# Routed experts in groups of four 32-slot tiles: 26 groups for 28, and a second PSUM bank for combine

## The chip, the cores and the metric

The kernel runs on one core of one Trainium2 chip. The metric is the device time of one execution in microseconds (us). Three runs of the kernel before took 1636.47, 1637.51 and 1638.44 us; the median is 1637.51. A profile was taken of one further execution, and all rows below are from it.

## The reference, cut to what matters

The reference is two transformer blocks on 256 tokens of width 1024, all in float32. The first block ends in a mixture of experts, and only that part is touched here:

```python
scores = sigmoid(xt @ w_router)                      # 256 tokens, 64 experts
choice = scores + router_bias                        # best 4 of 8 groups of experts, then top 8 experts
wts    = scores[eidx] / sum * 2.5                    # 8 weights per token: 2048 assignments
for each expert e, on the rows routed to it:
    ye = (silu(x @ w_gate_e[e]) * (x @ w_up_e[e])) @ w_down_e[e]     # 1024 -> 256 -> 1024
    routed[rows] += ye * w
return routed + swiglu(xt, w_gate_sh, w_up_sh, w_down_sh)            # a shared expert for all tokens
```

Each expert has 1 MB of gate and up weights for the first half of the width, 1 MB for the second, and 1 MB for down: 192 MB for the 64. The counts of tokens per expert are known only when the router has run. The second block has attention over a memory (its values need a projection of 256 by 1024, `mem_v`) and a second mixture of 16 larger experts, whose weights (about 200 MB) are streamed at the end of the kernel.

## The kernel before, in words

**Sorting the experts.** The kernel ranks the 64 experts by their counts on the chip: a position for each, the largest counts first. Four experts (0, 1, 62 and 63, `FIRST`) are put ahead of all others, since their weights are loaded while the router still works. The capacity of a position is fixed when the kernel is built: 64 slots for the first four, 128 for the next four (`N1`), 64 for the next 32 (`N2`), 32 for the remaining 24. If an expert has more tokens than its position has slots, a flag turns on a branch (lines 1137 to 1178) that runs all 64 experts once more on what was left over.

**Groups.** TensorE's 128 columns are 128 slots. A group fills them with one expert of 128 slots, two of 64 or four of 32, placed side by side by `tile_position`. There are 4 groups of one expert, 18 of two and 6 of four, 28 in all. `_group_pairs` puts them into 14 pairs and sets the order: the four pairs that come first have two experts in each of their groups (groups 0 to 7), then pairs of a four with a one and pairs of two twos take turns. The order on TensorE is the order of the code (`manual_schedule`).

**One group** (class `Group`, lines 960 to 1064, called from the loop at 1084) does this on TensorE: `gate_up` (line 1021; 8 steps over the width, each with one matmul for each tile, N = 512, into the single bank u); then the four quarters of `combine` of the group before (lines 1054 and 1055, bank c, which DVE adds into `y1` at line 1064), mixed with the gather of half of the next pair's rows (lines 956 and 957, bank g, copied by ScalarE), the transpose of the activations (`flip`, line 1032), `place` (line 991, which slot each token takes) and `weigh` (line 1003, the routing weight of each slot), these three in bank t; then `down` (line 1045, two halves in the two y banks), whose result ScalarE and DVE split into a high and a low part (lines 214 and 215).

**Spare work.** Work that no group needs at once is a generator, `pieces`, that issues one matmul for each step: the shared expert's gate (16 steps), the memory values `mem_v` (64 steps, line 731), the shared expert's up (16) and down (16). Twenty steps are issued during the routing, five while the first pair is gathered, and the rest by `piece(fills)` at two places in each group's middle; `FILL` says how many at each: none in a group of one expert, 2 in a group of two, 4 in a group of four. Their bank is d, of which there is one; line 735 (ScalarE) or line 749 (DVE) empties it.

**Loads.** SP issues the expert weights in 1 MB transfers (line 929) in the order in which groups need them: the first halves of the group's gate/up weights, the second halves, the down weights. They go to a ring of buffers ("lanes"), ten at first. A load waits until TensorE's last matmul on the buffer's old contents is done. `pieces` hands over more buffers when their contents are no longer needed: two after `mem_v`, two after the shared up, one after the shared down. The loads of group i+1 stand ahead of group i's matmuls in the code. When the last group's loads are issued, five loads of the next block's `w_in2` follow them on the same queue (line 1096). Three transfers of 1 MB for the spare work are issued by ScalarE's queue ("park", line 652).

The eight PSUM banks of this stage are d 1, t 2, g 1, u 1, y 2, c 1.

Of the kernel before, what the change touches and what calls it, by code (L numbers as in the profile page):

```python
# [21 lines left out]
P = 128  # L22
# [6 lines left out]
FILL = {1: 0, 2: 2, 4: 4}  # L29


# [3 lines left out]
NF, N1, N2 = len(FIRST), 4, 32  # L35
CAP1, CAP2, CAP4 = 128, 64, 32


def _group_pairs():
    s = [(NF + i, 1) for i in range(N1)]  # L40
    p = [(2 * i, 2) for i in range(NF // 2)] + [(NF + N1 + 2 * i, 2) for i in range(N2 // 2)]
    q = [(NF + N1 + N2 + 4 * i, 4) for i in range((N_EXP - NF - N1 - N2) // 4)]
    out = []
    while s or p or q:
        g = []
        for lst in (p, p) if len(out) < 4 or not q or (len(out) % 2 and len(p) - 2 >= len(q) - len(s)) else (q, s or p):
            if lst:
                g.append(lst.pop(0))
        if g:
            out.append(g)  # L50
    return out
# [4 lines left out]
def body(tc, I, out):  # L56
# [76 lines left out]
    slotc = lambda n: col("iotac" if n == 1 else f"slot{n}", 1)  # L133
    own = lambda n: col(f"own{n}", 2 * n)
# [561 lines left out]
    open_banks(b2, "b2", d=1, t=2, g=1, u=1, y=2, c=1)  # L696
# [7 lines left out]
    def shared(ps, w, a):  # L704
        w = w.rearrange("p (k n) -> p k n", k=KD)
        for k in range(KD):
            nc.tensor.matmul(ps[:, :T + 1], w[:, k, a * P:(a + 1) * P], hx[:, k], start=(k == 0), stop=(k == KD - 1))
            yield
# [11 lines left out]

    mem_v = None

    def values():
        nonlocal mem_v
        mem_v = big(5, [P, 2, D], F32, "mem_v")
        for c in range(4):
            w = parked.popleft().rearrange("p (k n) -> p k n", k=KD)
            for b in range(2):
                ps = bank("d")
                for k in range(KD):  # L730
                    nc.tensor.matmul(ps[:, :256], hm[:, k, b * P:(b + 1) * P], w[:, k], start=(k == 0),
                                     stop=(k == KD - 1))
                    if k < KD - 1:
                        yield
                nc.scalar.activation(mem_v[:, b, 256 * c:256 * c + 256], ps[:, :256], AF.Copy, scale=rmc[:, b:b + 1])
                if b == 0:
                    yield
            yield park

    def shared_down():  # L740
        w = parked.popleft().rearrange("p (f n) -> p f n", f=2)
        for j in range(4):
            ps = bank("d").rearrange("p (a t) -> p a t", a=2)
            for a in range(2):
                o = (2 * j + a) * P
                for f in range(2):
                    nc.tensor.matmul(ps[:, a], w[:, f, o:o + P], sgl[:, f], start=(f == 0), stop=(f == 1))
                    yield
            nc.vector.tensor_add(y1[:, 2 * j:2 * j + 2], ps, y1[:, 2 * j:2 * j + 2])

    def pieces():
        for a in range(2):
            yield from shared(gate[a], shg, a)
        yield from values()
        add_lanes(2, 10)
        w = parked.popleft()
        for a in range(2):
            ps = bank("d")
            yield from shared(ps, w, a)
            shared_act(1, a, ps)  # L760
        add_lanes(11, 7)
# [16 lines left out]
    for b in range(2):  # L778
        for q in range(2):
            ps = bank("cdug"[2 * b + q])  # L780
# [142 lines left out]
    groups = [(i0, n, pi, g) for pi, gp in enumerate(GROUP_PAIRS) for g, (i0, n) in enumerate(gp)]  # L923
# [8 lines left out]
    def slots(pi):  # L932

        G = pe.tile([P, 2, 2, P], F32R, name="G", tag="G")
        for g, (i0, n) in enumerate(GROUP_PAIRS[pi]):
            cap = P // n
            for b in range(2):
                last = nc.vector.tensor_tensor(
                    G[:, b, g].rearrange("p (e s) -> p e s", e=n),
                    iota[:, None, :cap].to_broadcast([P, n, cap]),  # L940
                    rkS[:, b, i0:i0 + n, None].to_broadcast([P, n, cap]), op=ALU.is_equal)
# [18 lines left out]
    class Group:  # L960


        def __init__(self, i, i0, n, pi, g):
            self.i, self.i0, self.n, self.pi, self.g = i, i0, n, pi, g
            self.cap = P // n

        def tp(self, j):
            return dict(tile_position=(0, self.cap * j)) if self.n > 1 else {}

        def load(self):  # L970
            self.regs, self.gu, self.wd = [], [], []
            if self.i0 < NF:
                es = FIRST[self.i0:self.i0 + self.n]
# [4 lines left out]
            for j in range(self.n):  # L978
                with tc.issue_after(issued[-8]) if len(issued) >= 8 else nullcontext():
                    self.regs.append(nc.sync.value_load(idx[0:1, self.i0 + j:self.i0 + j + 1], min_val=0, max_val=63))  # L980
                first.append(eload(I["w_gu"], self.regs[j], 0))
# [3 lines left out]
        def place(self):  # L985

            i0, n, cap = self.i0, self.n, self.cap
            ps = bank("t")
            for j in range(n):
                c = permb[:, i0 + j:i0 + j + 1]  # L990
                nc.tensor.matmul(ps[cap * j:cap * (j + 1), :T],
                                 bass.AP(tensor=c.tensor, offset=c.offset, ap=[c.ap[0], [0, cap]]), rkTb,
                                 start=True, stop=True, **self.tp(j))
            self.S = pe.tile([P, T], F32R, name="S", tag="S")
            nc.vector.tensor_scalar(self.S, ps[:, :T], slotc(n), 0.0, op0=ALU.is_equal, op1=ALU.add)

        def weigh(self):

            i0, n = self.i0, self.n
            G = Gs[self.pi][:, :, self.g]  # L1000
            ps = bank("t")
            for b in range(2):
                nc.tensor.matmul(ps[:, :2 * n], G[:, b], wS[:, b, i0:i0 + n].rearrange("p e u -> p (e u)"),
                                 start=(b == 0), stop=(b == 1))
            self.wsl = pe.tile([P, 1], F32, name="wsl", tag="wsl")
            if n > 1:
                wm = pe.tile([P, 2 * n], F32, name="wm", tag="wm")
                nc.vector.tensor_mul(wm, ps[:, :2 * n], own(n))
                nc.vector.reduce_sum(self.wsl, wm, axis=AX)
            else:  # L1010
                nc.vector.reduce_sum(self.wsl, ps[:, :2], axis=AX)

        def gate_up(self):
            cap = self.cap
            xg = xg_of[self.pi][:, :, self.g * P:(self.g + 1) * P]
            pg = bank("u")
            for half in range(2):
                ws = [w.rearrange("p (k n) -> p k n", k=4) for w in self.gu[half]]
                for k in range(4):
                    for j in range(self.n):  # L1020
# [15 lines left out]
        def down(self):  # L1036
            cap = self.cap
# [3 lines left out]
            for h in range(2):  # L1041
                py = bank("y")
                for f in range(2):
                    for j in range(self.n):
                        nc.tensor.matmul(py[cap * j:cap * (j + 1)], self.aT[:, f, cap * j:cap * (j + 1)],  # L1045
                                         wd[j][:, f, h * 512:(h + 1) * 512], start=(f == 0), stop=(f == 1),
                                         **self.tp(j))
# [28 lines left out]
    with tc.manual_schedule(engines={mybir.EngineType.PE}):  # L1076
# [5 lines left out]
        piece()  # L1082
        gr[0].weigh()
        for i, u in enumerate(gr):
# [23 lines left out]
            fills = FILL[u.n]  # L1108

# [6 lines left out]
            piece(fills)  # L1116
# [7 lines left out]
            piece(fills)  # L1124
# [611 lines left out]
def layout(inp):  # L1736
# [47 lines left out]
    for n in (2, 4):  # L1784
        cap = P // n
        addv(f"slot{n}", (pidx % cap)[:, None].astype(np.float32))
        addv(f"own{n}", (pidx[:, None] // cap == np.arange(2 * n)[None] // 2).astype(np.float32))
# [49 lines left out]
```

## Time and profile before

| | us |
|---|---|
| median of three runs | 1637.51 |
| profiled execution | 1637.62 |
| its span, first to last instruction | 1635.8 |
| TensorE busy (PE) | 1419.8 |
| VectorE busy (DVE) | 615.4 |
| ScalarE busy (ACT) | 431.8 |
| moved by DMA | 524.76 MB, 321 GB/s over the span |

How to read it: the span leaves out 1.8 us before the first and after the last instruction. PE's busy time counts modelled ends of pipelined matmuls, so how long a step took is read from the start of one instruction to the start of the next. The granted clock is a share of 2.4 GHz; 0.50 is 1.2 GHz. The routed experts take the stretch from 318 us (the first `gate_up`) to 818 us (the end of the last `down`); the first mixture's routing lies just before, the second block after it.

### The profile page before, as it was taken

What the parts mean: (1) busy time and instruction counts of PE and PEld (TensorE: products, weight loads), DVE (VectorE), ACT (ScalarE), POOL (GpSimd) and SP (SyncE); (2) the same over time, 40 slices, a digit from 0 to 9 for tenths busy, and PEclk for the clock granted to TensorE, in tenths of its full rate; (3) what the DMA queues carried; (4) which work ended last, traced back from release to release, by engine and by line L of the source; (5) the groups of instructions that cost most, each with busy time, mean ns of one, the idle gap of its engine ahead of it and who ended that gap; (6) DMA issues with size and microseconds to landing.
All of it is one profiled execution on the core that took longest, in us unless ns stands there. A gap on an engine that the chain in (4) does not pass through costs nothing. (4 is left out here: it accounts for less than half of the span.)

```text
span 1635.8 us, 23949 instructions
## 1 busy us (share of the span) xinstructions
PE 1419.8 (87%) x9780; PEld 903.9 (55%) x9780; DVE 615.4 (38%) x1111; ACT 431.8 (26%) x756; POOL 101.8 (6%) x155
## 2 busy tenths in 40 slices
PE   6999999899999999999878999999796767777664
PEld 5778898554555555444378889999441121121121
DVE  6433654532223233333376566675321111111112
ACT  4453454211111111112165444454210000000001
POOL 1010101200000000000021110011200000000001
PEclk9999999999999999999988999999899777777876
DMA  8885746198999999999944345575399999999995
GB/s 327 340 348 211 297 167 223 68 376 342 383 390 403 416 418 421 415 420 420 420 162 143 115 143 203 196 284 217 140 420 421 421 421 420 421 421 421 421 421 215
DMA packets 74161, 524.76 MB, mean 321 GB/s; under 512 B 8282, under 2 KB 9890, under 8 KB 10562
## 3 DMA queue, kind: packets, MB, share of 16 engines
q1 hardware_dynamic: 72848, 519.35, 79.1%
q10 hardware_dynamic: 1202, 3.87, 0.6%
q8 instruction: 77, 1.26, 0.3%
q14 instruction: 34, 0.28, 0.0%
HBM read 521.01 MB, written 2.17 MB: 320 GB/s over the span
## 5 line engine op out<-in xcount | busy, mean ns | idle before, releaser
L215 DVE TENSOR_TENSOR whl<-w,whl 128x1024 fp32r<-128x1024 f32 x156 | 195.5, 1257 | 143.1 <-ACT whl L214 140.5
L221 PE MATMUL ps_d<-h_hi,whl 128*128 128x256 f32 x1216 | 225.6, 284 | 1.1 <-ACT whl L214 1.1
L214 ACT CAST whl<-w 128x1024 fp32r<-128x1024 f32 x156 | 162.8, 1048 | 167.5 <-PE ps_d L221 141.1
L1021 PE MATMUL ps_u<-w,xg 128*64 128x512 f32 (+2 forms) x1024 | 200.5, 594 | 3.1 <-DMA w<-in_w_gu 3.1
L221 PEld LDWEIGHTS ps_d<-h_hi,whl 128*128 128x128 f32 x1216 | 189.2, 189 | 6.8 <-ACT whl L214 2.8
L221 PE MATMUL ps_d<-h_lo,whl 128*128 128x256 f32 x608 | 171.6, 282 | 0.0
L1586 PE MATMUL ps_u<-w,xgb 128*32 128x512 f32 x512 | 95.7, 822 | 51.1 <-DMA w<-in_w_gu 51.1
L1021 PEld LDWEIGHTS ps_u<-w,xg 128*64 128x64 f32 (+2 forms) x1024 | 64.9, 130 | 134.9 <-issue 127.2
L221 PEld LDWEIGHTS ps_d<-h_lo,whl 128*128 128x128 f32 x608 | 114.2, 188 | 1.5 <-issue 1.3
L1586 PE MATMUL ps_u<-w,xga 128*32 128x512 f32 x512 | 95.7, 708 | 19.1 <-DMA w<-in_w_gu 19.0
L1655 PE MATMUL ps_y<-w,aT 128*32 128x256 f32 x1024 | 84.3, 470 | 28.6 <-DMA w<-in_w_down 24.4
L1045 PE MATMUL ps_y<-w,aT 128*64 128x512 f32 (+2 forms) x512 | 105.0, 605 | 0.0
L1054 PE MATMUL ps_c<-S,yy 128*128 128x256 f32 x224 | 74.0, 352 | 20.9 <-DVE y L1064 13.3
L1064 DVE TENSOR_TENSOR y<-ps_c,y 128x512 f32<-128x512 f32 x100 | 68.6, 686 | 53.2 <-PE ps_c L1055 53.2
L1643 DVE SCALAR_TENSOR_TENSOR act<-ps_u,wsl,sl 128x256 f32<-128x256 f32 x16 | 7.7, 483 | 211.8 <-ACT sl L1633 211.8
L1586 PEld LDWEIGHTS ps_u<-w,xgb 128*32 128x32 f32 x512 | 12.7, 124 | 123.7 <-DMA w<-in_w_gu 118.0
L1027 DVE SCALAR_TENSOR_TENSOR act<-ps_u,wsl,sl 128x256 f32<-128x256 f32 x28 | 13.6, 484 | 176.5 <-ACT sl L1025 176.5
L1633 ACT ACTIVATE sl<-ps_u 128x256 f32<-128x256 f32 x16 | 6.1, 383 | 275.2 <-PE ps_u L1586 275.1
L1655 PEld LDWEIGHTS ps_y<-w,aT 128*32 128x32 f32 x1024 | 33.5, 129 | 74.9 <-DMA w<-in_w_down 44.2
L1054 PEld LDWEIGHTS ps_c<-S,yy 128*128 128x128 f32 x224 | 42.8, 191 | 50.3 <-issue 21.2
L214 ACT CAST yy<-ps_y 128x512 fp32r<-128x512 f32 x56 | 32.8, 585 | 116.0 <-PE ps_y L1045 116.0
L215 DVE TENSOR_TENSOR yy<-ps_y,yy 128x512 fp32r<-128x512 f32 x56 | 38.7, 691 | 57.7 <-ACT yy L214 57.7
(493 smaller groups left out, 2281.7 us busy)
## 6 DMA issues: line engine op xcount, KB each, us to landing
w<-in_w_gu SPq DMA_DIRECT2D x256, 1024.0 KB, 16.3
w<-in_w_down_e SPq DMA_DIRECT2D x64, 1024.0 KB, 11.0
w<-in_w_down SPq DMA_DIRECT2D x64, 1024.0 KB, 19.8
w<-in_w_in SPq DMA_DIRECT2D x42, 1024.0 KB, 6.2
w<-in_w_ada SPq DMA_DIRECT2D x24, 1024.0 KB, 10.0
w<-in_w_mem_kv SPq DMA_DIRECT2D x4, 1024.0 KB, 13.9
w<-in_w_out SPq DMA_DIRECT2D x4, 1024.0 KB, 7.3
w<-in_w_conv_out SPq DMA_DIRECT2D x4, 1024.0 KB, 4.9
```

The lines of the kernel that those rows point to most:

```text
L214: nc.scalar.copy(hi, src)
L215: eng.tensor_sub(lo, src, hi.bitcast(F32))
L221: nc.tensor.matmul(region, l, r, start=(start and u == 0), stop=(stop and u == 2), skip_group_check=True)
L1021: nc.tensor.matmul(pg[cap * j:cap * (j + 1)], xg[:, 4 * half + k, cap * j:cap * (j + 1)], ws[j][:, k], start=(half == 0 and k == 0), stop= ...
L1027: nc.vector.scalar_tensor_tensor(self.act, pg[:, 256:], self.wsl, sl, op0=ALU.mult, op1=ALU.mult)
L1045: nc.tensor.matmul(py[cap * j:cap * (j + 1)], self.aT[:, f, cap * j:cap * (j + 1)], wd[j][:, f, h * 512:(h + 1) * 512], start=(f == 0), st ...
L1054: nc.tensor.matmul(ps[:, a], self.yy[:, 0, k * P:(k + 1) * P], self.S, start=True, stop=False)
L1064: nc.vector.tensor_add(y1[:, 2 * q:2 * q + 2], ps, y1[:, 2 * q:2 * q + 2])
L1586: mm = nc.tensor.matmul(pg[32 * j:32 * j + 32], xg[k][:, 32 * e:32 * e + 32], w[:, 512 * j:512 * j + 512], start=(k == 0), stop=(k == KD - ...
L1633: silu = nc.scalar.activation(sl, pg[:, :256], AF.Silu)
L1643: nc.vector.scalar_tensor_tensor(act, pg[:, 256:], wsl[:, e % 4, e // 4:e // 4 + 1], sl, op0=ALU.mult, op1=ALU.mult)
L1655: nc.tensor.matmul(py[32 * j:32 * j + 32, :256], aT[:, f, 32 * v:32 * v + 32], w[:, f, 256 * j:256 * j + 256], start=(v == 0 and f == 0), ...
```

## The change

1. Positions and capacities: four experts with 96 slots for four with 128, and 28 with 64 slots for 32. The four smallest experts (positions 60 to 63) are taken out of the groups of four.
2. Groups: a group's tiles are 32 or 64 columns. A group of the new kind holds one expert with three 32-slot tiles, which use the same weights, and one of the four smallest experts in the fourth. There are 16 groups of two 64-slot experts (two of them the resident ones), 4 of the new kind and 6 of four experts: 26.
3. Order: the resident pair, then six pairs that begin with a group of four (with the four new groups and two groups of two), then six pairs of two twos.
4. Banks: d is gone, c has two. Spare work uses the c banks until the first group has been weighed, and the y banks from then on.
5. Spare work: each group issues 4 pieces at both places, whatever it holds; one piece that stood between `place` and `weigh` of group 0 is gone; the generator's stops are moved so that 8 pieces (or 4) always finish a bank.

```diff
-NF, N1, N2 = len(FIRST), 4, 32
-CAP1, CAP2, CAP4 = 128, 64, 32
+NF, N1, N2 = len(FIRST), 4, 28
+CAP1, CAP2, CAP4 = 96, 64, 32
...
+    n4 = NF + N1 + N2
+    first = [[(2 * i, 2), (2 * i + 1, 2)] for i in range(NF // 2)]
+    three = [[(NF + i, 3), (N_EXP - N1 + i, 1)] for i in range(N1)]
+    two = [[(NF + N1 + 2 * i, 2), (NF + N1 + 2 * i + 1, 2)] for i in range(N2 // 2)]
+    one = [[(n4 + 4 * i + j, 1) for j in range(4)] for i in range((N_EXP - N1 - n4) // 4)]
+    more = three + two
+    out = [first]
+    while more or one:
+        out.append(([one.pop(0)] if one else [more.pop(0)]) + ([more.pop(0)] if more else []))
...
-    open_banks(b2, "b2", d=1, t=2, g=1, u=1, y=2, c=1)
+    open_banks(b2, "b2", t=2, g=1, u=1, y=2, c=2)
...
-                ps = bank("d")
+                ps = bank(spare)
...
+                for i0, n, cap in ([(exps[0][0], len(exps), 32 * exps[0][1])] if exps[0][1] < 3 else
+                                   [(i, 1, 32 * t) for i, t in exps]):
+                    last = nc.vector.tensor_tensor(
+                        G[:, b, g, o:o + n * cap].rearrange("p (e s) -> p e s", e=n),
...
+            for j, (_, t) in enumerate(exps):
+                self.tiles += [(j, o + u, w) for u in range(0, 32 * t, w)]
+                o += 32 * t
...
-                    for j in range(self.n):
-                        nc.tensor.matmul(pg[cap * j:cap * (j + 1)], xg[:, 4 * half + k, cap * j:cap * (j + 1)],
-                                         ws[j][:, k], start=(half == 0 and k == 0), stop=(half == 1 and k == 3),
-                                         **self.tp(j))
+                    for j, o, w in self.tiles:
+                        nc.tensor.matmul(pg[o:o + w], xg[:, 4 * half + k, o:o + w], ws[j][:, k],
+                                         start=(half == 0 and k == 0), stop=(half == 1 and k == 3),
+                                         tile_position=(0, o))
...
         gr[0].place()
-        piece()
         gr[0].weigh()
+        spare = "y"
...
-            fills = FILL[u.n]
...
-            piece(fills)
+            piece(4)
```

`place`, `weigh` and `down` loop over the same tiles; `weigh` reads the weights of its two experts with a stride where their positions lie apart. The tables `slot` and `own` get a third kind for the new groups.

## Rows read from the trace of the kernel before

**Rows 1.** The page's 40 equal slices of the span, busy share in tenths.

```profile
PE   6999999899999999999878999999796767777664
DMA  8885746198999999999944345575399999999995
```

**Rows 2.** Stretches: length, busy us of each engine (instructions), granted clock, DMA share, GB/s.

```profile
318.00:350.00 32.00, 30.95 (x168) 16.21 (x166) 7.19 (x19) 5.94 (x12) 0.00 (x0) 1.00 0.68 272
450.00:500.00 50.00, 47.32 (x281) 25.14 (x279) 14.78 (x31) 9.17 (x18) 0.00 (x0) 1.00 0.96 396
550.00:650.00 100.00, 95.69 (x526) 52.35 (x523) 31.56 (x67) 17.41 (x34) 0.00 (x0) 1.00 1.01 419
...
325.00:807.00 482.00, 456.91 (x2667) 241.49 (x2666) 153.30 (x330) 85.88 (x169) 0.00 (x0) 1.00 0.98 401
1200.00:1600.00 400.00, 286.43 (x2088) 85.48 (x2080) 61.17 (x107) 16.06 (x43) 0.00 (x0) 0.78 1.01 421
```

**Rows 3.** Waits of the load queue, 318 to 807: total us, times, longest.

```profile
SPq L929 <- PE ps_y L1045: 215.9, 25, 10.5
SPq L929 <- PE ps_u L1021: 98.1, 44, 16.7
```

**Rows 4.** TensorE in time, last groups: start us, us, what [idle before <-releaser].

```profile
782.58 3.62 PE L1021 MATMUL ps_u<-w,xg 128*32 128x512 f32 x26 [1.45 <-DMA w<-in_w_gu]
...
802.47 3.65 PE L1021 MATMUL ps_u<-w,xg 128*64 128x512 f32 x14 [1.27 <-DMA w<-in_w_gu]
...
807.89 0.39 PE L1054 MATMUL ps_c<-S,yy 128*128 128x256 f32 x1 [1.11 <-DVE xT L1059]
...
812.95 5.44 PE L1045 MATMUL ps_y<-w,aT 128*64 128x512 f32 x16
```

**Rows 5.** TensorE in order of time, one group of two without spare work.

```profile
727.85 7.04 PE L1021 MATMUL ps_u<-w,xg 128*64 128x512 f32 x32
...
738.13 0.36 PE L1054 MATMUL ps_c<-S,yy 128*128 128x256 f32 x1 [0.44 <-DVE y L1064]
...
740.42 3.65 PE L1045 MATMUL ps_y<-w,aT 128*64 128x512 f32 x16
...
744.00 1.06 PE L1021 MATMUL ps_u<-w,xg 128*32 128x512 f32 x8
```

**Rows 6.** Groups of instructions, shapes apart: busy us, mean ns | idle before.

```profile
L1021 PE MATMUL ps_u<-w,xg 128*64 128x512 f32 x576 | 128.3, 594 | 1.6 <-DMA w<-in_w_gu 1.6
...
L1064 DVE TENSOR_TENSOR y<-ps_c,y 128x512 f32<-128x512 f32 x100 | 68.6, 686 | 53.2 <-PE ps_c L1055 53.2
...
L1021 PE MATMUL ps_u<-w,xg 128*32 128x512 f32 x384 | 43.7, 594 | 1.4 <-DMA w<-in_w_gu 1.4
...
L1021 PE MATMUL ps_u<-w,xg 128*128 128x512 f32 x64 | 28.5, 599 | 0.0
...
L938 DVE TENSOR_TENSOR G<-c_vec,rkS 128x128 fp32r<-128x128 f32 x56 | 13.0, 283 | 0.0
```

**Rows 7.** TensorE in order of time: group 0's down, and spare work.

```profile
329.18 3.65 PE L1045 MATMUL ps_y<-w,aT 128*64 128x512 f32 x16
...
395.12 1.02 PE L731 MATMUL ps_d<-wx,hm 128*128 128x256 f32 x4
395.80 0.47 PE L1054 MATMUL ps_c<-S,yy 128*128 128x256 f32 x1
...
417.61 0.70 PE L731 MATMUL ps_d<-wx,hm 128*128 128x256 f32 x2 [0.62 <-ACT mem_v L735]
```

**Rows 8.** Issues on the load queue in time: start us, us, what.

```profile
324.69 9.08 SPq L929 DMA_DIRECT2D w<-in_w_gu  x4
...
775.18 7.81 SPq L929 DMA_DIRECT2D w<-in_w_gu  x4
```

**Rows 9.** The page's DMA issues: count, KB each, median us to landing.

```profile
w<-in_w_conv_out SPq DMA_DIRECT2D x4, 1024.0 KB, 4.9
```

**Rows 10.** The stretch in which the clock fell, columns as in rows 2.

```profile
809.80:816.50 6.70, 5.73 (x18) 2.75 (x20) 2.88 (x5) 1.04 (x1) 0.00 (x0) 0.50 1.02 423
```

More of the change, by code (lines that the diff above doesn't have):

```diff
@@ L132, in body @@
     iotac = col("iotac", 1)
-    slotc = lambda n: col("iotac" if n == 1 else f"slot{n}", 1)
-    own = lambda n: col(f"own{n}", 2 * n)
+    slotc = lambda n: col(f"slot{n}", 1)
+    own = lambda n: col(f"own{n}", 8 if n == 4 else 4)
     before = const.tile([P, T], BF16, name="before")
@@ L742, in shared_down @@
         for j in range(4):
-            ps = bank("d").rearrange("p (a t) -> p a t", a=2)
+            ps = bank(spare).rearrange("p (a t) -> p a t", a=2)
             for a in range(2):
@@ L757, in pieces @@
         for a in range(2):
-            ps = bank("d")
+            ps = bank(spare)
             yield from shared(ps, w, a)
             shared_act(1, a, ps)
+            yield
         add_lanes(11, 7)
@@ L922, in body @@
     xgs, yys = deque((3, 4)), deque((14, 15))
[L923 removed]
+    groups = [(exps, pi, g) for pi, gp in enumerate(GROUP_PAIRS) for g, exps in enumerate(gp)]
     issued, silu, Gs, xg_of = [], [], {}, {}
@@ L1002, in weigh @@
             for b in range(2):
-                nc.tensor.matmul(ps[:, :2 * n], G[:, b], wS[:, b, i0:i0 + n].rearrange("p e u -> p (e u)"),
-                                 start=(b == 0), stop=(b == 1))
+                nc.tensor.matmul(ps[:, :2 * n].rearrange("p (e u) -> p e u", u=2), G[:, b],
+                                 wS[:, b, i0:i1 + 1:(i1 - i0) // (n - 1)], start=(b == 0), stop=(b == 1))
             self.wsl = pe.tile([P, 1], F32, name="wsl", tag="wsl")
[L1006 to L1011, printed above, removed]
+            wm = pe.tile([P, 2 * n], F32, name="wm", tag="wm")
+            nc.vector.tensor_mul(wm, ps[:, :2 * n], own(self.kind))
+            nc.vector.reduce_sum(self.wsl, wm, axis=AX)
         def gate_up(self):
-            cap = self.cap
             xg = xg_of[self.pi][:, :, self.g * P:(self.g + 1) * P]
@@ L1043, in down @@
                 for f in range(2):
[L1044 to L1047, printed above, removed]
+                    for j, o, w in self.tiles:
+                        nc.tensor.matmul(py[o:o + w], self.aT[:, f, o:o + w], wd[j][:, f, h * 512:(h + 1) * 512],
+                                         start=(f == 0), stop=(f == 1), tile_position=(0, o))
                 split(py, self.yy[:, 0, h * 512:(h + 1) * 512], self.yy[:, 1, h * 512:(h + 1) * 512])
@@ L1123, in body @@
                 gather(pn, gs_[1])
-            piece(fills)
+            piece(4)
             c(3)
@@ L1783, in layout @@
     addv("iotac", pidx[:, None].astype(np.float32))
[L1784 to L1787, printed above, removed]
+    for n, starts in ((2, (0, 64)), (3, (0, 96)), (4, (0, 32, 64, 96))):
+        e = np.searchsorted(starts, pidx, side="right") - 1
+        addv(f"slot{n}", (pidx - np.array(starts)[e])[:, None].astype(np.float32))
+        addv(f"own{n}", (e[:, None] == np.arange(2 * len(starts))[None] // 2).astype(np.float32))
     addv("iota", np.broadcast_to(np.arange(P, dtype=np.float32), (P, P)))
```

72 lines of the change are left out of this document (32 added, 40 removed).

## The prediction

> **What bounds the kernel now.** I began with the page's slices: TensorE is busy 0.9 or more through the middle of the span while the DMA engines go from 0.9 to full [rows 1]. The change touches the routed experts, so I cut out their stage, 318 to 818 us. The view by stretches [rows 2] shows two limits that nearly meet. Up to 550 us TensorE is busy about 95% of the time and the DMA engines have room (0.68 at first, 0.96 later); from 550 us on the DMA engines are full at 419 GB/s, with TensorE as busy. Which of them ends last is told by the waits. The load queue spent 314 us in wait for TensorE's last use of a buffer (215.9 + 98.1) and little for anything else [rows 3]: a load leaves when a ring buffer comes free, so TensorE sets the pace. Only the last two groups wait for data, 1.45 us at 782.58 and 1.27 at 802.47 [rows 4]. So TensorE bounds this stage up to about 776 us, and DMA stands right behind it: over 325 to 807 us it moved 401 GB/s where it moves 421 in the last phase, when it is the limit alone [rows 2]; that is 20/421 x 482 = 23 us of idle DMA. That is all that faster TensorE work can win here, if no group is loaded later than now.
>
> **One group's work.** A group of two experts without spare work runs from its gate/up at 727.85 to the next at 744.00, 16.15 us: gate/up 7.0, then a middle of 5.5 (combine of the group before, gather, flip, place, weigh, from 734.9 to 740.42), then down 3.6 [rows 5]. What decides the case is that this hardly depends on what the group holds: gate/up takes 128.3/18 = 7.1 us with two 64-slot tiles, 43.7/6 = 7.3 with four 32-slot tiles (waits for data included), 28.5/4 = 7.1 with one of 128 [rows 6]. So a group with one expert, of which there were four, costs TensorE as much as one with four.
>
> **Edits, one by one.**
> *28 groups to 26.* Two groups go: 2 x 16 = 32 us of TensorE work. The 180 loads of non-resident experts stay 180.
> *The 96+32 groups.* Three tiles that share one expert's weights are not in the trace. By the nearest rows, four tiles of 32 and one tile of 128, gate/up is 7.1 to 7.3 us [rows 6]: no difference either way; I take 0. Weigh reads its weights with a stride now; it lies in the middle's 5.5 us with as many columns, so 0, and by the spread of the rows for gate/up 0.1 us either way. Each of the four groups adds two writes of G, 0.28 us of DVE work apiece [rows 6], beside TensorE's gate/up; with that cover gone 4 x 2 x 0.28 = 2.2 us.
> *Two combine banks.* Quarter 2 of a combine now waits 0.44 us for DVE to empty the only bank [rows 5]. With two banks quarter 0's is long empty. DVE's 0.69 us for a quarter [rows 6] then stands beside flip, place and gather. Bounds: 0 (something else late, such as the gather's one bank) to the 0.45 with restart; I take 0.45, so a group costs 15.7 us.
> *Spare work.* 88 pieces at 0.34 us (two from 395.12 to 395.80, [rows 7]) are left when the groups begin, 30 us, before and after. They now come eight to a group in groups 0 to 10 (2.7 us each), where before they were spread over 0 to 20. In the y banks they avoid the 0.62 us that some waited for the single d bank [rows 7]; bounds 0.6 won or, if down finds the bank not yet emptied, 0.6 lost a group. Both lie under DMA, below, so I count 0. One piece fewer ahead of group 0 starts it 0.3 us earlier. Spare work done sooner also gives its five buffers to the ring sooner (groups 7, 9 and 11; before 12, 16 and 20).
> *The order.* Before, eight groups of two experts came first. Now groups 2 to 13 alternate four experts (12 loads) with two (6), and groups 14 to 25 have two each.
>
> **The sum.** A 1 MB load takes 2.49 us when DMA is full (four issues, three steps, in 7.81 us at 775.18, the last one taking 0.34 itself, [rows 8]); alone it lands 4.9 us after issue [rows 9].
> Stage A, groups 2 to 13: 18 loads a pair, 44.9 us, against TensorE's 2 x (15.7 + 2.7) = 36.8. DMA is the bound from here, and TensorE waits 8 us a pair. The first load leaves when group 0's gate/up is done, 324.7 now [rows 8], 324.4 then, and lands at 329.3. 108 expert loads and the 3 parked ones: 110 x 2.49 = 273.9 more. DMA idles where buffers are not free yet: two free at 324.4, the next two when group 0's down ends. Its middle, 324.7 to 329.18 now with four pieces [rows 7], gets four more, 5.9 us: 324.4 + 5.9 + 3.6 = 333.9, so the next load lands at 338.8 where 334.3 was possible, 4.5 us lost, and about 1 us when group 1's down frees the next pair. Afterwards each load in my bookkeeping is issued before DMA has worked off the one ahead. Last landing of stage A: 329.3 + 273.9 + 5.5 = 608.7. Group 13's second gate/up half can start two loads earlier, at 603.7: + 3.5 + 5.1 + 3.5 = 615.8 at the end of its down.
> Stage B, groups 14 to 25: TensorE 15.7 a group against 6 x 2.49 = 14.9, so TensorE leads, narrowly. 10 x 15.7 + 2 x 13.8 (the last pair gathers nothing, 16 matmuls of 0.12 us less) = 184.6: the last down ends at 800.4. Its loads are there by 608.7 + 72 x 2.49 = 788.0, 9 us ahead of need.
> Before, it ends at 812.95 + 5.44 = 818.4 [rows 4]. The gain is 18.0 us. Nothing behind the stage holds the end in place: the five early loads of the next block follow the experts' at once, and the last phase runs on DMA from whenever its buffers come free. The profiled execution took 1637.62 us (span 1635.8), the median of the runs is 1637.51, so the two are the same; 1637.6 - 18.0 = 1619.6, rounded to 1620. Cross-check from the other limit: 23 us of idle DMA less the 5.5 us that stay leave 17.5.
>
> **The clock.** In the last two groups the granted clock fell to 0.50 (1.2 GHz) at 809.8 us, after waits of 1.27 and 1.11 us (and shorter ones) had come close together, and down took 5.44 us for 3.65 [rows 4, 5, 10]; one wait of 1.45 us at 782.58 had not lowered it. Stage A has 8 us of waits a pair in my sum, most of it in the four-expert group's gate/up. The Trainium skill (TensorE: Matmul & The Clock Gate, section HAM oscillation) tells of a matmul kernel whose DMA waits dropped the clock at every K tile, so that each restarted at half rate; the rows of the last phase here agree, with 0.78 granted over 1200 to 1600 us, where TensorE is busy for 286 of 400 us [rows 2]. Yet there DMA stays at 421 GB/s. A fall costs nothing while it fits into the 8 us of slack a pair. Stage B has no waits, so no fall in my sum.
>
> **Rivals.**
> *The clock eats the gain (slower).* Place: groups 2 to 13. If stage A falls a little below the last phase's 0.78 [rows 2], to 0.76, a pair costs 36.8/0.76 = 48.4 us, 3.5 over DMA's 44.9; six pairs lose 21 us: 1641. It decides below 0.82 (36.8/44.9), and wipes the gain out at 0.77. For: waits of several us are likely in every pair. Against: in the last phase TensorE has less to do (286 of 400 us; here 36.8 of 44.9), and the falls follow waits. 6%. By the Trainium skill's case (same page and section), every restart at half rate, half a gate/up (3.5 us, [rows 5]) would be doubled once a pair, which stays inside the slack of 8 us and leaves 1620.
> *The ring starves DMA.* Ten buffers, twelve loads in a four-expert group: two downs must wait until its own first gate/up half frees buffers. The trace has this once, at groups 8 and 9, with DMA at 0.96 [rows 2]. If every such group up to 10 costs 2.5 us of idle DMA (one load), five give 12: 1632. Against: at the time of those issues DMA has four to six loads queued. 14%.
> *Two combine banks win nothing.* Stage B at 16.15: 12 x 0.45 = 5.4 us: 1625. 10%, within the forecast's side.
> *It doesn't do what it says:* an expert over its capacity would run the fallback over all 64 experts. The reference's routing of its inputs gives 75, 66, 65, 65 for the four largest (96 slots), then 61 to 29 (64), then 28 down to 8 (32); none overflows. 1%.
> *DMA floor:* if stage B is quicker than I think, DMA ends it: 788.0 + 3.6 + 2 for landing and start = 793.6, so 818.4 - 793.6 = 24.8 us: 1613. 8%.
>
> **Chances.** Forecast within 5 us 55%, the banks' rival 10, the floor 8, starved ring 14, clock 6, overflow 1, and 6 for what I don't see, 4 of it no change. This kernel's runs spread by 0.1%, and 0.2% (3.3 us) is what counts as a change. Faster: 55 + 10 + 8 + 14 = 87%. Same 4%, slower 6 + 1 + 2 = 9%. The range leaves out a tenth at each end: 1611 (just under the floor) to 1633 (the starved ring).
>
> **What would show it.** Right: 26 gate/up groups; DMA at 1.0 from about 352 us on instead of 550; waits of TensorE for w_gu in groups 4 to 12, none from 14 on; periods of 15.7 us in stage B and no wait for L1064's adds; the last down near 800 us. Wrong: DMA under 0.97 between 360 and 600 (ring), clock under 0.82 there (clock), periods of 16.1 in stage B (banks). The forecast falls if groups 2 to 13, from group 2's gate/up near 352 us to 615.8, take more than 275 us.

## The result, and the profile after

| | before, us | after, us |
|---|---|---|
| median (runs) | 1637.97 (1636.47 to 1639.04, 4) | 1613.78 (1612.59 to 1615.48, 4) |
| profiled execution, its span | 1637.62, 1635.8 | 1615.48, 1613.8 |
| first gate/up to end of last down | 500.8 | 482.0 |

The ratio is 0.9854, interval [0.9837, 0.9871]: 24 us faster. Forecast were 1620 in 1611 to 1633. The sign came out as said and the time lies in the range, but 6 us below 1620, at the 1613 that the prediction gave to its DMA-floor rival (8%). Three terms of the sum were off, and the experiments show that one part of the change, the two groups fewer, was worth nothing.

The page of the kernel after, two of its rows of 40 slices, to set beside [rows 1]:

```profile
PE   5999999799999989999989999999797776776774
DMA  7985755379999999999944345566499999999995
```

DMA is at 9 from the tenth slice (363 us) to the end of the stage, where the tenth had an 8 before; tenths hide the rest of the difference, so it is read from the stretches. The stretches of the kernel after, columns as in [rows 2]:

```profile
350.00:400.00 50.00, 47.01 (x350) 24.15 (x352) 13.87 (x32) 8.80 (x17) 0.00 (x0) 0.97 0.95 389
450.00:500.00 50.00, 44.09 (x314) 22.20 (x318) 11.91 (x27) 6.68 (x13) 0.00 (x0) 0.95 1.01 419
325.00:807.00 482.00, 455.92 (x2852) 233.05 (x2846) 151.00 (x335) 87.08 (x164) 0.00 (x0) 0.97 1.00 412
...
353.50:357.30 3.80, 3.80 (x32) 0.99 (x32) 1.38 (x2) 0.86 (x2) 0.00 (x0) 1.00 0.35 82
...
637.00:773.00 136.00, 136.00 (x773) 70.01 (x770) 48.13 (x102) 27.94 (x54) 0.00 (x0) 1.00 1.01 420
...
382.00:386.00 4.00, 4.00 (x22) 0.89 (x14) 0.00 (x0) 0.00 (x0) 0.00 (x0) 0.57 1.01 420
805.50:812.30 6.80, 3.65 (x16) 3.63 (x17) 6.17 (x15) 4.21 (x12) 0.66 (x6) 0.50 0.93 364
```

Between 450 and 500 us the DMA share is 1.01 where [rows 2] had 0.96, and TensorE is the one that idles. From 637 to 773 both are full. The short row from 353.50 and the last two are used below; the last two are stretches in which the granted clock fell, one in the stage and one behind it. The load queue's waits, as in [rows 3], say the same: it now waits mostly for earlier loads to land, and much less for TensorE to free a buffer (143 us instead of 314).

```profile
SPq L931 <- DMA w<-in_w_gu: 130.2, 70, 2.7
SPq L931 <- PE ps_y L1049: 86.1, 16, 10.7
SPq L931 <- PE ps_u L1026: 56.8, 23, 15.8
```

Three of the queue's issues, and the time from issue to landing of the last of them, the two down loads of the last group (columns as in [rows 8] and [rows 9]):

```profile
326.33 17.67 SPq L931 DMA_DIRECT2D w<-in_w_gu  x8
354.88 4.83 SPq L931 DMA_DIRECT2D w<-in_w_down_e  x4
...
773.37 2.78 SPq L931 DMA_DIRECT2D w<-in_w_down_e  x2
...
w<-in_w_down_e SPq DMA_DIRECT2D x2, 1024.0 KB, 19.8
```

The stage's last load leaves at 775.8 (773.37 + 2.78 less the 0.34 of one issue) and lands 19.8 us later, at 795.6. The last down starts 1.9 us behind that landing and ends 5.6 us behind it, at 801.20.

TensorE of the kernel after in order of time, columns as in [rows 4]: gate/up of a four-expert group (group 12), a group of two (group 20, answers to [rows 5]), and the end of the stage.

```profile
577.72 1.06 PE L1026 MATMUL ps_u<-w,xg 128*32 128x512 f32 x6
579.73 3.63 PE L1026 MATMUL ps_u<-w,xg 128*32 128x512 f32 x28 [0.96 <-DMA w<-in_w_gu]
584.73 1.05 PE L1026 MATMUL ps_u<-w,xg 128*32 128x512 f32 x2 [1.37 <-DMA w<-in_w_gu]
587.23 1.91 PE L1026 MATMUL ps_u<-w,xg 128*32 128x512 f32 x2 [1.45 <-DMA w<-in_w_gu]
589.65 5.68 PE L1026 MATMUL ps_u<-w,xg 128*32 128x512 f32 x26 [0.51 <-DMA w<-in_w_gu]
...
712.81 7.04 PE L1026 MATMUL ps_u<-w,xg 128*64 128x512 f32 x32
719.78 0.38 PE L1057 MATMUL ps_c<-S,yy 128*128 128x256 f32 x1
...
721.30 0.28 PE L1057 MATMUL ps_c<-S,yy 128*128 128x256 f32 x1
...
722.31 0.38 PE L1057 MATMUL ps_c<-S,yy 128*128 128x256 f32 x1
...
724.51 3.65 PE L1049 MATMUL ps_y<-w,aT 128*64 128x512 f32 x16
728.00 0.59 PE L1026 MATMUL ps_u<-w,xg 128*64 128x512 f32 x1
...
797.55 3.65 PE L1049 MATMUL ps_y<-w,aT 128*64 128x512 f32 x16
...
804.68 0.28 PE L1058 MATMUL ps_c<-S,yy 128*128 128x256 f32 x1
808.65 0.79 PE L217 MATMUL ps_s<-h_hi,whl 128*128 128x256 f32 x2 [3.69 <-ACT h_hi L1193]
```

Group 12's gate/up takes 17.6 us where the work is 7.05. Eight groups up to 13 wait like this, and their gate/ups are 53 us longer together; from group 14 on gate/up takes 7.04 (7.18 at the first, 7.23 at the last) and a period, from one gate/up to the next, is 15.19 (712.81 to 728.00; 16.15 in [rows 5]).

Two readings of the kernel before that the prediction lacked are needed below. First, its weight loads (PEld) at quarters 1 and 2 of one combine, the same group as [rows 5]; the third line is the load at quarter 2 in the kernel after:

```profile
736.51 0.19 PEld L1054 LDWEIGHTS ps_c<-S,yy 128*128 128x128 f32 x1 [0.22 <-DVE y L1064]
...
738.10 0.19 PEld L1054 LDWEIGHTS ps_c<-S,yy 128*128 128x128 f32 x1 [0.60 <-ACT aT L1034]
...
722.31 0.19 PEld L1057 LDWEIGHTS ps_c<-S,yy 128*128 128x128 f32 x1
```

The mark of 0.60 names ScalarE's copy, but the load doesn't need it: in the kernel after, the same load starts at 722.31 without idle time, while that copy (722.25 to 722.62) still runs. DVE's add, which empties the bank, ended at 737.98.

Second, its TensorE in order of time: quarters 0 and 1 of that combine, then the end behind the last down.

```profile
734.82 0.39 PE L1054 MATMUL ps_c<-S,yy 128*128 128x256 f32 x1
...
736.52 0.39 PE L1054 MATMUL ps_c<-S,yy 128*128 128x256 f32 x1
...
820.91 0.39 PE L1054 MATMUL ps_c<-S,yy 128*128 128x256 f32 x1 [1.85 <-DVE xT L1059]
...
822.92 0.36 PE L1054 MATMUL ps_c<-S,yy 128*128 128x256 f32 x1 [1.27 <-DVE xT L1059]
...
824.66 0.58 PE L1054 MATMUL ps_c<-S,yy 128*128 128x256 f32 x1 [0.97 <-DVE xT L1059]
...
825.47 0.41 PE L1055 MATMUL ps_c<-S,yy 128*128 128x256 f32 x1
827.60 0.80 PE L221 MATMUL ps_s<-h_hi,whl 128*128 128x256 f32 x2 [1.72 <-ACT h_hi L1192]
```

### The profile page after: what moved, and what is told of

Read it like the earlier page. It is cut to its first block, busy times and chain, and to the rows that moved or that the text cites. A ratio compares the mean times of both kernels' runs of the same rounds, so it can differ in the third digit from the quotient of the medians.

```text
span 1613.8 us, 24163 instructions
## 1 busy us (share of the span) xinstructions
PE 1406.1 (87%) x9908; PEld 888.3 (55%) x9908; DVE 603.7 (37%) x1099; ACT 426.3 (26%) x744; POOL 104.7 (6%) x155
## 4 chain that ended last, share of the span: by engine, by line
DMA 24%; PE 21%; DVE 2%; issue 2%; ACT 2%; POOL 0%; DVEq 0%; SPq 0%; ACTq 0%; POOLq 0%
DMA w<-in_w_gu 14%; PE ps_d L217 13%; DMA w<-in_w_down 10%; PE ps_u L1587 2%; PE ps_s L217 1%; PE ps_y L1656 1%; PE ps_s L1366 1%; PE ps_s L1365 1%; PE ps_t L1373 0%; PE ps_t L1356 0%; ACT whl L210 0%; ACT L170 0%; DVE whl L211 0%; PE ps_c L1666 0%; PE ps_s L1490 0%
## 5 line engine op out<-in xcount | busy, mean ns | idle before, releaser
L1026 PE MATMUL ps_u<-w,xg 128*32 128x512 f32 (+1 forms) x1152 | 214.1, 635 | 22.4 <-DMA w<-in_w_gu 22.4
L1026 PEld LDWEIGHTS ps_u<-w,xg 128*32 128x32 f32 (+1 forms) x1152 | 63.8, 127 | 167.8 <-issue 122.4
L1587 PE MATMUL ps_u<-w,xgb 128*32 128x512 f32 x512 | 92.1, 793 | 56.4 <-DMA w<-in_w_gu 56.4
L1656 PE MATMUL ps_y<-w,aT 128*32 128x256 f32 x1024 | 88.1, 492 | 23.6 <-DMA w<-in_w_down 19.9
L1049 PE MATMUL ps_y<-w,aT 128*32 128x512 f32 (+1 forms) x576 | 94.9, 597 | 0.0
L1634 ACT ACTIVATE sl<-ps_u 128x256 f32<-128x256 f32 x16 | 6.1, 384 | 275.5 <-PE ps_u L1587 275.4
L1067 DVE TENSOR_TENSOR y<-ps_c,y 128x512 f32<-128x512 f32 x92 | 63.0, 686 | 32.4 <-PE ps_c L1058 32.4
L1030 ACT ACTIVATE sl<-ps_u 128x256 f32<-128x256 f32 x26 | 10.0, 385 | 217.1 <-PE ps_u L1026 217.1
L1057 PE MATMUL ps_c<-S,yy 128*128 128x256 f32 x208 | 62.9, 325 | 1.1 <-ACT whl L210 0.6
L1058 PE MATMUL ps_c<-S,yy 128*128 128x256 f32 x208 | 53.8, 281 | 0.5 <-DVE yy L211 0.5
## 6 DMA issues: line engine op xcount, KB each, us to landing
w<-in_w_gu SPq DMA_DIRECT2D x256, 1024.0 KB, 19.8
w<-in_w_down_e SPq DMA_DIRECT2D x64, 1024.0 KB, 19.8
w<-in_w_down SPq DMA_DIRECT2D x64, 1024.0 KB, 19.8
w<-in_w_mem_kv SPq DMA_DIRECT2D x4, 1024.0 KB, 13.5
```

The lines of the kernel that those rows point to most:

```text
L1026: nc.tensor.matmul(pg[o:o + w], xg[:, 4 * half + k, o:o + w], ws[j][:, k], start=(half == 0 and k == 0), stop=(half == 1 and k == 3), tile ...
L1049: nc.tensor.matmul(py[o:o + w], self.aT[:, f, o:o + w], wd[j][:, f, h * 512:(h + 1) * 512], start=(f == 0), stop=(f == 1), tile_position=( ...
L1057: nc.tensor.matmul(ps[:, a], self.yy[:, 0, k * P:(k + 1) * P], self.S, start=True, stop=False)
L1058: nc.tensor.matmul(ps[:, a], self.yy[:, 1, k * P:(k + 1) * P], self.S, start=False, stop=True)
L1067: nc.vector.tensor_add(y1[:, 2 * q:2 * q + 2], ps, y1[:, 2 * q:2 * q + 2])
L1587: mm = nc.tensor.matmul(pg[32 * j:32 * j + 32], xg[k][:, 32 * e:32 * e + 32], w[:, 512 * j:512 * j + 512], start=(k == 0), stop=(k == KD - ...
```

## The experiments

In all of them "stage" is the time from the first gate/up to the end of the last down. The diffs are against the kernel after, but for the first (against the kernel before) and the fifth (against the first). The theory (T1): the order keeps DMA full from about 352 us, the second combine bank lets TensorE keep up behind it, and each needs the other.

**One part alone: the banks.** The 28 groups and the order of before, with the new banks and spare work.

```diff
-    open_banks(b2, "b2", d=1, t=2, g=1, u=1, y=2, c=1)
+    open_banks(b2, "b2", t=2, g=1, u=1, y=2, c=2)
...
-            fills = FILL[u.n]
+            fills = 4
```

> The old 28 groups in their old order, with the new banks (two for combine, spare work in y) and four pieces of spare work at both places of every group. Theory 1 (two limits in turn: TensorE's time counts only where DMA is not full, and the old order asks for few loads in the first 150 us): groups become about 0.95 us shorter, but DMA still idles early, the last down ends about 8 us sooner than before, the tail behind it 4 us shorter: 1626 us. Rival (TensorE bounded the old stage, so each 0.95 us counts, 28 times, and the tail on top, up to the 23 us of idle DMA): 1612 to 1614 us, the whole gain. If the banks are worth nothing: 1638.

1630.18 us, ratio 0.9954 [0.9940, 0.9968], stage 497.5; the runs of the kernel before beside it had a median of 1636.65. That is 4 us above the theory's 1626 and far from the rival's 1612 to 1614. Two stretches of the kernel before, then the same two of this run:

```profile
350.00:400.00 50.00, 48.09 (x268) 26.42 (x265) 14.87 (x30) 9.13 (x19) 0.00 (x0) 1.00 0.91 366
400.00:450.00 50.00, 48.52 (x269) 25.45 (x267) 15.76 (x37) 8.71 (x17) 0.00 (x0) 1.00 0.92 369
...
350.00:400.00 50.00, 50.00 (x274) 28.04 (x270) 13.64 (x29) 9.30 (x18) 0.00 (x0) 1.00 0.88 352
400.00:450.00 50.00, 50.00 (x273) 28.35 (x274) 15.64 (x36) 9.77 (x19) 0.00 (x0) 1.00 0.86 346
```

The early idle of DMA stays, and is even larger than before, since eight spare pieces stand in every early group. The time that the banks save late is then spent in waits for data: gate/up of groups 16, 20 and 24 to 27 takes 9.6, 13.0, 13.2, 10.5, 16.6 and 10.0 us. The stage ends 5.6 us behind its last landing (808.0), as in the kernel after. The banks alone are worth some 7 of the 24 us (7.5 by the ratio, 6.5 by the medians).

**The other part alone: groups and order,** with one c bank and one d bank as before.

```diff
-    open_banks(b2, "b2", t=2, g=1, u=1, y=2, c=2)
+    open_banks(b2, "b2", d=1, t=2, g=1, u=1, y=2, c=1)
...
-    spare = "c"
+    spare = "d"
...
-        spare = "y"
```

> The new 26 groups in the new order, with the old banks: one for combine, one (d) for spare work. Theory 1: stage A (groups 2 to 13) stays bound by DMA and ends where it does with the new banks; groups 14 to 25 take about 16.1 us instead of 15.2 (about 11 us more) and the tail 4 us more: 1628 to 1630 us. Rival (the banks did it): 1635 or more.

1635.68 us, ratio 0.9989 [0.9979, 0.9998]. I had expected 1628 to 1630, so this missed, on the rival's side. DMA is full from 400 us as in the kernel after:

```profile
400.00:450.00 50.00, 44.72 (x328) 22.19 (x320) 11.16 (x26) 7.14 (x14) 0.00 (x0) 0.97 1.01 419
...
773.36 2.78 SPq L931 DMA_DIRECT2D w<-in_w_down_e  x2
...
794.40:797.80 3.40, 3.40 (x12) 2.05 (x14) 2.86 (x8) 0.00 (x0) 0.00 (x0) 0.50 0.96 398
```

Group 13's down ends at 622.3, within 1 us of the kernel after; from there a group takes 16.03 to 16.07 us, and the last pair 17.6 and 19.4, with the granted clock at 0.50 (1.2 GHz) in part of it, after waits for the one bank. The expectation had priced that last pair like the other groups. The last load leaves at the same 775.8 as in the kernel after and lands 19.8 us later as there, but the stage ends 24.0 us behind it, at 819.6, and is as long as before (500.9): here TensorE is late, not DMA. Regrouping and reordering without the second bank gained 1 to 2 us (0.3 to 3.4 by the interval).

**Only the second combine bank taken back.** Spare work stays in the y banks.

```diff
-    open_banks(b2, "b2", t=2, g=1, u=1, y=2, c=2)
+    open_banks(b2, "b2", d=1, t=2, g=1, u=1, y=2, c=1)
...
-    spare = "c"
+    spare = "d"
```

> The changed kernel with a single combine bank and spare work in y; the eighth bank serves spare work only before group 0 is weighed. It parts the second combine bank from the move of the spare work. Theory 1: the same as with all old banks, 1628 to 1630 us, since the waits of spare work lie under DMA. Rival (spare work's single bank cost something): 2 us or more faster than that.

1634.22 us, ratio 0.9988 [0.9978, 0.9997]; missed as the run before. The stage is 498.3, 16.3 more than the kernel after: 1.2 up to group 14, ten times 0.83 in groups 14 to 23, 6.8 in the last pair; the stretch behind it is 3.6 longer too. TensorE at one middle:

```profile
710.67 0.36 PE L1057 MATMUL ps_c<-S,yy 128*128 128x256 f32 x1 [0.43 <-DVE y L1067]
```

Spare work's move to the y banks shows no gain: both runs start group 14 303.5 us after the first gate/up, and the 2.6 us between their stages (498.3 against 500.9) arise in the last pair, where no spare work is left and the two do the same. The second combine bank is worth about 20 us of the 24, once the order is there (1634.22 - 1613.78), more than half of it in the last pair and behind it.

**Only the order taken back:** the six pairs of twos first, the pairs with fours behind them; groups and banks of the kernel after.

```diff
+    rest = []
     while more or one:
-        out.append(([one.pop(0)] if one else [more.pop(0)]) + ([more.pop(0)] if more else []))
+        rest.append(([one.pop(0)] if one else [more.pop(0)]) + ([more.pop(0)] if more else []))
+    out += rest[6:] + rest[:6]
```

> The changed kernel with its pairs in another order: the six pairs of two twos right after the resident pair, the six pairs with a group of four behind them. Same groups, loads, banks. Theory 1: twelve groups bound by TensorE come first while DMA idles, then twelve bound by DMA: last down about 22 us later, 1636 us, nearly all of the gain gone. Rival (the number of groups and the banks decide, their order does not): 1614 us.

1636.44 us, ratio 0.9995 [0.9985, 1.0004]: as expected, the whole gain is gone. Its stretches, then TensorE at gate/up of group 16:

```profile
350.00:400.00 50.00, 50.00 (x271) 27.39 (x268) 14.18 (x31) 9.28 (x18) 0.00 (x0) 1.00 0.88 351
400.00:450.00 50.00, 50.00 (x275) 28.96 (x275) 15.79 (x36) 9.74 (x19) 0.00 (x0) 1.00 0.86 349
```

```profile
596.85 1.25 PE L1028 MATMUL ps_u<-w,xg 128*32 128x512 f32 x6
599.55 3.63 PE L1028 MATMUL ps_u<-w,xg 128*32 128x512 f32 x28 [1.45 <-DMA w<-in_w_gu]
```

TensorE never waits up to 550 us, DMA does; behind it the fours come, and the gate/up of the first group of each pair from group 16 on takes 18 to 20 us. The same groups and the same banks in another order are worth nothing.

**The order and the banks without the regrouping:** 28 groups with the old capacities, the heavy pairs ahead.

```diff
+    out = [[p.pop(0), p.pop(0)]]
     while s or p or q:
...
+        out.append([(q or p).pop(0), (s or p).pop(0)])
```

> 28 groups with the old capacities (four groups of one expert, 18 of two, six of four), but in the new kind of order (the resident pair, four pairs of a four and a one, two pairs of a four and a two, then seven pairs of two twos) and with the new banks and spare work. It has the 28 TensorE groups of the kernel before and everything else of the kernel after. T1 (what counts is that DMA is kept full from about 352 us and that the second combine bank then lets TensorE keep up; the two groups fewer are hidden, since a pair with a one has three loads fewer for the same TensorE work and its time comes out of DMA's stretch): stage A is four pairs of 15 loads (37.4 us) and two of 18 (44.9), 239.5 us for 269.5, stage B is one pair longer, 2 x 15.2 = 30.4: stage 482 to 485 us, 1614 to 1617. Rival T2 (the two groups fewer are a large part of the gain: 2 x 15.2 us of TensorE, of which at least a third shows): 1625 or more, with TensorE and not w_gu as the limit in the pairs with a one.

1614.19 us (1612.73 to 1615.36), ratio 0.9860 [0.9843, 0.9876], stage 481.9: the kernel after to within 1 us, with the 28 groups of the kernel before. Its stretches:

```profile
400.00:450.00 50.00, 48.55 (x301) 29.09 (x300) 14.99 (x33) 9.42 (x20) 0.00 (x0) 1.00 1.01 419
...
600.00:767.00 167.00, 167.00 (x950) 85.77 (x948) 60.14 (x131) 34.15 (x66) 0.00 (x0) 1.00 1.01 420
```

DMA is full with TensorE waiting less (its gate/ups are 21 us longer by waits, where the kernel after has 53), and from group 14 on the period is 15.20. The two groups fewer only lengthened TensorE's waits. From the first gate/up to the last landing it takes 476.3 us, the kernel after 476.4, and both stages end 5.6 us behind that.

**How much TensorE has in hand.** Groups of four use their first half's gate/up weights for both halves, so 24 loads fewer are issued.

```diff
-            self.gu = [first, [eload(I["w_gu"], r, 1) for r in self.regs]]
+            self.gu = [first, first if self.kind == 4 else [eload(I["w_gu"], r, 1) for r in self.regs]]
```

> The changed kernel with 24 loads fewer: groups of four experts use the first half of their gate/up weights for the second half too (that half is left out). TensorE does the same work. Theory (stage A is bound by DMA, 44.9 us of loads a pair; with 14 loads, 34.9 us, it is bound by TensorE): the waits for weights in groups 3 to 13 go nearly all, about 50 us of them, the stage shortens by 35 to 48 us: 1566 to 1580 us. Rival (stage A is bound by TensorE or by the ring's hand-over of buffers): 1600 us or more.

1563.28 us, ratio 0.9547 [0.9531, 0.9563], stage 428.7; 50 us for 24 loads, a little beyond the expected range. Every gate/up takes 7.04 to 7.09 us. The stretch that idled most in the kernel after has none of it:

```profile
450.00:500.00 50.00, 50.00 (x404) 29.64 (x400) 17.76 (x40) 8.14 (x17) 0.00 (x0) 1.00 0.99 396
```

TensorE's own 26 groups need 429 us, and 28 would need some 459 (429 + 2 x 15.2, an estimate); the loads need 476 up to the last landing, as just read. Both fit under the loads, which is why 26 or 28 is the same.

**The second bank at the very end.** The combines of the last two groups go through the one g bank.

```diff
-            ps = bank("c").rearrange("p (a t) -> p a t", a=2)
+            ps = bank("g" if last else "c").rearrange("p (a t) -> p a t", a=2)
```

> The changed kernel, but the last two combines (those that add into x directly) use one bank, g, which is idle by then; the others keep two. With a single bank throughout, group 25 took 4.2 us longer and the last combine 3.4 us. Theory (each quarter waits for DVE's two adds of 0.48 us, and the clock falls after such waits): 6 to 8 us slower than the changed kernel, 1620 to 1622 us. Rival (the tail is bound by DVE's adds anyway): within 1 us of it.

1622.29 us, ratio 0.9907 [0.9894, 0.9921]: hit. TensorE of this run behind its last down:

```profile
806.67 0.39 PE L1057 MATMUL ps_g<-S,yy 128*128 128x256 f32 x1
...
808.96 0.39 PE L1057 MATMUL ps_g<-S,yy 128*128 128x256 f32 x1 [1.56 <-DVE xT L1062]
...
810.98 0.36 PE L1057 MATMUL ps_g<-S,yy 128*128 128x256 f32 x1 [1.27 <-DVE xT L1062]
```

The waits of the kernel before are back, the middle of group 25 is 6.41 us instead of 3.23, its down 6.04 instead of 3.65 at a granted clock of 0.50, and the combine ends 7.14 us after the last down instead of 3.75. Two of 26 combines carry 6.9 us (against 1615.37 for the kernel after on the same chip, below) to 8.5 us (against 1613.78).

**Spare work out of the groups in which DMA starts,** in two forms; the kernel after ran again beside them. The first form changes both calls of `piece(4)`; the second also moves the last pair with a group of four, groups 12 and 13, to places 20 and 21.

```diff
-            piece(4)
+            piece(4 if i > 1 else 0)
...
+    g = out.pop(6)
+    out.insert(10, g)
```

> The changed kernel itself, beside the three that follow on the same chip: 1613 to 1615 us, ratio 0.985 to before.

> The changed kernel with no spare work in groups 0 and 1: it starts in group 2 and ends in group 12. Theory (in stage A TensorE's spare work lies under DMA, except in groups 0 and 1, where it holds back the ring's first buffers): buffers come free 3.4 us earlier behind group 0 and 6.9 us behind group 1, DMA idles about 4 us less before 352 us, all that follows moves with it: 3 to 4 us faster than the changed kernel, 1610 us. Rival (the end is set by TensorE's own sum of work, which stays the same): 1613 to 1615.

> The same, and the last group of four experts moved from group 12 to group 20. Theory: the wait of 10 us that stands ahead of stage B in group 12 goes, DMA bounds up to group 20 and TensorE's lag behind DMA at the end (about 10 us between the last landing and the last down's end, 3.6 of them the down) shrinks by 2 us: 1608 us. Rival (more work behind a late heavy group): as e_spare_late or slower.

The kernel after: 1615.37 us, ratio 0.9867 [0.9851, 0.9882], stage 481.7. Without spare work in groups 0 and 1: 1611.38 us, 0.9851 [0.9836, 0.9866], stage 478.2. With the last four-expert group moved to place 20 as well: 1611.95 us, 0.9846 [0.9833, 0.9860], stage 479.1; that step, expected to give 1608, gave nothing. It counted on a TensorE that ends about 10 us behind the last landing; the trace has 5.6 in all three runs, so there was nothing to shrink. In the first form the stage is 3.5 us shorter, as the theory has it, and DMA is at 1.01 over 350 to 400 us where the kernel after has 0.95; the intervals of the whole runs overlap, so the first form is the best kernel here by its median only. Its stretch:

```profile
350.00:400.00 50.00, 44.42 (x322) 22.70 (x318) 11.17 (x26) 7.16 (x14) 0.00 (x0) 0.94 1.01 419
```

**Ten ring buffers to the end,** none handed over by the spare work.

```diff
-        add_lanes(2, 10)
...
-        add_lanes(11, 7)
...
-        add_lanes(16)
...
                 piece(1000)
+                add_lanes(2, 10, 11, 7, 16)
```

> The changed kernel with ten ring buffers to the end of the expert stage: the five that spare work frees join only ahead of the last group's following loads. Theory (ten are enough: loads are asked for early enough, DMA is full from 352 us on): within 2 us of the changed kernel, 1613 to 1616 us. Rival (the ring starves DMA; the earlier growth of the ring is part of the gain): 1620 us or more.

1614.09 us, ratio 0.9859 [0.9843, 0.9876], stage 482.3: nothing lost. The five buffers more do not matter here, so the rival of a starved ring is out.

## Why the prediction was right, and where its terms were off

- **What bounds the kernel:** right up to group 13, not behind it. TensorE led before and DMA stood 23 us behind; after, DMA is full from about 357 us (forecast 352; 0.35 from 353.5 to 357.3, 1.01 from 400 on), and TensorE waits for w_gu in eight groups up to 13. "TensorE leads, narrowly" for groups 14 to 25 failed: with a period of 15.2 against 15.1 for six loads (72 loads between the landings at 614.6 and 795.6) TensorE falls back by 0.1 us a group, the lighter group 24 (13.5 us) wins that back, and the last gate/up is 0.2 us longer (7.23) for the load of its second half. The stage ends 5.6 us behind the last landing, in this run and in the seven others here that have two combine banks throughout and all loads, whatever their groups, order and ring. So DMA ends it.
- **Stage A:** the step "Last landing of stage A: 608.7 ... 615.8 at the end of its down" was 3.9 us short. Group 13's down ends 302.4 us after the first gate/up (621.64 - 319.22), forecast 298.5. The mis-sized term is the "about 1 us when group 1's down frees the next pair": no load leaves between 344.0 and 354.88, when that down has ended, and DMA idles 2.5 us of the 3.8 behind 353.50. "I count 0" for spare work holds for its banks, but not for its place: in groups 0 and 1 it holds back these buffers, which the sum priced for group 0 alone, and without it there the stage is 3.5 us shorter. Loads at 419 GB/s instead of the 421 of a load in 2.49 us make another 1.3 us (an estimate, 273.9 x 2/421); the last 1 us is not traced.
- **Stage B:** the step "I take 0.45, so a group costs 15.7 us" is the mis-sized one: the period is 15.2 and the saving 0.83 (from the run with the single bank put back). I took the bank's price from the matmuls' wait alone, 0.44 in [rows 5]. The weight load that goes before each matmul has to be counted too: at quarter 1 the load waited 0.22 for DVE while the matmul behind it carried no mark, and at quarter 2 it waited 0.60 where its matmul is marked with 0.44; 0.22 + 0.60 = 0.82. Counted from the first combine matmul, quarter 1 starts 0.18 us earlier now (1.52 for 1.70), quarter 2 0.78 earlier (2.53 for 3.31) [rows 5]. Ten groups at 0.5 below the forecast: 5 us, as much as brings TensorE to the pace of the loads. That weights are loaded ahead of matmuls still in flight is also what the Trainium skill states (Perfetto Trace Analysis, section Tensor Engine Instruction); the rows agree (for the matmul at 735.04 the load starts at 734.92, under the matmul of 734.82), and show that the load ahead is held with the bank.
- **The tail:** "Nothing behind the stage holds the end in place" was right, but the stretch behind it was counted as unchanged, and it became 4.8 us shorter (span less last down: 812.6 for 817.4). The combine of the last group alone waited 1.85, 1.27 and 0.97 us for DVE to empty the only bank; with two it ends 3.74 us earlier, and the next phase starts 1.76 earlier (7.45 us after the last down for 9.21). The rest is not traced to its end. In the first 80 to 85 us behind the stage the clock was at 0.50 for 20.5 us before and for 13.7 after; 6.8 us at half rate are worth 3.4 at most. But a second execution of the kernel after, with the same 13.7, took 814.1 for this stretch, so 1.5 of the 4.8 us can be the spread between executions.
- **The sum:** the first gate/up is 1.9 us late against the forecast (the work ahead of it began 2.5 late in this execution), stage A +3.9, stage B -5.0, tail -4.8: -4.0, and 1619.6 - 4.0 = 1615.6 for the profiled 1615.48. Errors of 4 to 5 us each cancelled in part. That the time met the DMA floor's 1613 is in part luck as well: its mechanism held, but the last landing came 7.6 us behind its 788.0, and the shorter tail, which it did not have, made up for 4.8 of them.
- **Rivals.** The clock: it fell in stage A, to 0.57 on the mean between 382 and 386 us and in five more places of 3.4 to 6.8 us, after waits for data, and cost nothing that shows, as DMA stayed at 419 GB/s: another execution of the same kernel, with two such falls in the stage for six, took 481.7 us for 482.0. The Trainium skill (TensorE: Matmul & The Clock Gate, section HAM oscillation) tells of a kernel that paid for each restart behind a DMA wait; the falls agree, the price does not, since here it lay under the next wait. The banks' rival is refuted by 0.83 us a group. The ring is refuted by ten buffers. DMA's floor, "if stage B is quicker than I think, DMA ends it", is what happened, and 8% was too little for it: its sum has 5.6 us from the last landing to the end of the last down, and 5.6 were measured.
- **Not seen:** the prediction calls "32 us of TensorE work" the first edit. In its own sum that number does nothing, since DMA sets stage A, and 28 groups in the new order would have come out the same; I didn't draw that conclusion. The run of 28 groups shows it. That order and banks are worth 2 and 7 us apart and 24 together was not forecast either: the order moves DMA's idle time out of the start, but the lead can be used only if the second half runs at DMA's pace of 15.1 us a group, and TensorE with one bank takes 16.05 and loses as much again in the last pair and behind it.

Still open: whether the kernel without early spare work is faster as a whole. Its stage is 3.5 us shorter and its median 4 us lower, but the intervals overlap; more runs would tell. Open too is what else than the combine shortens the stretch behind the stage.

## What to carry to other kernels

Where two limits nearly meet, list the work in which each leads: put the load-heavy groups first so that the transfers start full and never stop, and shorten the other engine's step in what follows; apart they gave 2 and 7 of the 24 us here. Then set the last landing against the end of the stage: a distance that stays the same from run to run (5.6 us here) says that the transfers end it, a longer one (24 us with one bank) that the engine does. Read the weight loads as well as the matmuls when you price a bank that is reused too soon, and look at the end of the stage by itself, where nothing hides the wait. Before counting work saved on one engine, ask which limit it lies under: two groups fewer, 30 us of TensorE, were worth nothing here.

## What the runs showed of the hardware that was not expected

A single PSUM bank between TensorE and DVE cost twice what the matmuls' waits show (0.83 us a group for 0.44), and the rows show the difference in the weight loads, which the bank's release holds too (0.22 and 0.60 us of idle time before them). And short falls of the granted clock to 1.2 GHz, six of 3.4 to 6.8 us inside the stage, cost nothing where the engine would have waited for data in any case; the same fall at the last group, where nothing is waited for, took down from 3.65 us to 6.04 in the run with the single bank at the end.
